# A two-layer gated-branch block with routed experts on one core: inputs laid out beforehand, router weights loaded at the layer's start, two more buffers for expert weights

## The chip, the core and the metric

The kernel runs on one core of one Trainium2 chip. The core has a matrix engine (PE, with its weight loads shown as PEld), three engines for element-wise work (DVE, ACT and POOL), a queue engine (SP) that issues most DMAs, and 16 DMA engines that move data between the chip's memory (DRAM) and the on-chip memory of 128 partitions. ACT and POOL can issue DMAs too; each issuing engine has its own queue. The metric is the device time of one execution in microseconds.

## The reference, cut to what matters

There are 256 latent tokens and 256 context tokens of width 1024, all in float32, and two layers. The second layer drops the context stream after its attention keys and values.

```python
for l in range(DEPTH):                                   # 2
    sh1, sc1, g1, sh2, sc2, g2 = split(silu(c) @ w_mod[l] + b_mod[l], 6)      # w_mod 1024 x 6144
    csh1, ..., cg2             = split(silu(c_ctx) @ w_mod[l] + b_mod[l], 6)
    p_x = modulate(rmsnorm(x, norm1_g[l]), sh1, sc1) @ w_in[l]                # w_in 1024 x 5376
    p_c = modulate(rmsnorm(ctx, norm1_g[l]), csh1, csc1) @ w_in[l]
    # three mixers on slices of p: windowed attention with a sink, depthwise conv of width 31, pooling
    x = x + g1 * merge_branches(...)                     # w_attn_o, w_conv_o, w_pool_o, gates, w_out
    # (context likewise in layer 0)
    h = modulate(rmsnorm(x, norm2_g[l]), sh2, sc2)
    aff = softmax(h @ w_router[l])                       # 16 experts
    g, idx = top_k(aff.T, 32)                            # each expert takes its 32 best tokens
    ye = (silu(xe @ w_e_gate) * (xe @ w_e_up)) @ w_e_down * g     # each matrix 1024 x 1024
    x = x + g2 * scatter_add(ye, idx)
return rmsnorm(x, final_norm_g)
```

The experts' weights are 16 x 3 x 4 MB per layer, 403 MB of the 530 MB that the kernel reads in all.

## The kernel before, in words

A tile framework keeps an order of priorities (mostly that of the program text), plans every engine's queue when the program is built, and places the waits. An instruction can therefore stand earlier in its queue than in the text, if its buffer was free in the planner's own clock. Each queue then runs strictly in order on the chip.

**Start.** L124 to L150 load the constants, c and c_ctx, the tokens and the small vectors, as rows which PE then turns into columns (L153, and `small_operands`, L168). `mod_first` (L371) computes shift and scale of layer 0's first norm in two halves of 512 columns each. A half reads four 1 MB tiles from the ring, each filled by two DMAs (L378) whose pieces are 2 KB long. Half 0 is needed for channels 0 to 3 of the normalized tokens, half 1 for channels 4 to 7 (`modulated`, L412).

**Mixers.** Weights come through a ring of five 1 MB buffers, tag `w` (`ring`, L103). `win` (L509) and `load` (L207) fetch 256 columns of w_in, in pieces of 1 KB; `qload` (L402) fetches q's columns in two DMAs with pieces of 512 bytes. ACT and DVE (or POOL) split each tile into a high and a low part (`split`, L214; buffers `ws`), and PE multiplies in three products (`mm3`, L490: its lines 494, 495 and 497). The later modulation matrices (`mod_group`, L227) are pumped in between these units. `layer_vectors` (L287) brings the conv taps and the sink. `merge` (L737) reads the three output projections, `project` (L863) reads w_out and adds the result to the stream.

**Routing.** `route` (L902) turns the tokens, multiplies them with the router weights `wr` and, for the part of the shift, with constant vectors (L905); softmax, top 32 by four rounds of max and replace, and one-hot matrices follow. `wr` stands in the tile `rt_` of the expert stage's memory (L852), is cleared by POOL (L854) and filled by two DMAs from ACT's queue (L855), in pieces of 64 bytes.

**Experts.** Each expert takes twelve loads of 1 MB: four of gate, four of up, four of down, in that order (`seq`, L331), with 8 KB per partition in one piece. `slot` (L310) hands out buffers in a fixed cycle: in layer 0 x0 to x3, once `y`, the five of the ring, two each of B, `A0`, `A1` and two of `ws`, 16 at first; in layer 1 also `xc`, `x4` and D, 19 in all. `prefetch` (L335) is called for two loads behind the attention of layer 1 and for two ahead of routing in both layers; `eload` (L352) asks for the others. PE computes gate and up (L1095), turns the hidden values (L1110), multiplies with down (L1118 in layer 0, L1123 in layer 1), and adds to the stream every four (layer 0) or two (layer 1) experts (L1140).

```python
order = ["x0", "x1", "x2", "x3"]
if last:
    order = ["xc", "A1"] + order + ["x4"] + ["w"] * RB + ["B", "B", "A0", "D", "D", "ws", "ws"]
else:
    order += ["w"] * RB + ["B", "B", "A0", "A1", "ws", "ws"]
```

## Time and profile before

| | us |
|---|---|
| median of 3 runs | 1751.48 (1750.38 to 1753.07) |
| the profiled execution | 1752.59 |
| its span in the trace | 1750.7 |
| PE busy | 1533.1 (88%) |
| DVE, ACT, POOL busy | 668.5, 408.1, 235.3 |
| DMA of the SP queue, share of 16 engines | 77.3% |
| mean granted PE clock | 0.955 |

Busy times are the union of an engine's instructions; a matmul's end is modelled, so a full PE is not PE at its peak. A float32 matmul has two records in the trace. The page cuts the span into 40 slices of 43.8 us; a digit is a busy share in tenths. A DMA share can exceed 1 a little, since packets overlap at their edges. In the chain of waits each piece is what released the next.

### The profile page before, as it was taken

Reading aid. Unit: us, or ns where it says so; the run is one execution under the profiler, and the core shown is the slowest. Engines: PE = TensorE matmul, PEld = TensorE weight load, DVE = VectorE, ACT = ScalarE, POOL = GpSimd, SP = SyncE. Lnnn points to the kernel's source line nnn. Section 1 sums busy time; section 2 is a strip of 40 time slices with the busy share of each in tenths; the row PEclk is TensorE's granted clock in tenths of the full one; section 3 lists DMA queues with packets and bytes.
Section 4 is the critical chain, followed back from the end, with each engine's and each line's share of the span. In section 5 each row is a group of like instructions: output and inputs, shape, how many; then the busy total and the mean of one; then the engine's idle time right before and its main releaser. Section 6 shows DMA issues by size and latency. Waiting matters only on the chain.

```text
span 1750.7 us, 19617 instructions
## 1 busy us (share of the span) xinstructions
PE 1533.1 (88%) x7794; PEld 825.5 (47%) x7794; DVE 668.5 (38%) x1145; ACT 408.1 (23%) x760; POOL 235.3 (13%) x242
## 2 busy tenths in 40 slices
PE   4999989999999999999999899999879676777675
PEld 2665567888654433433333376789743111111111
DVE  2568993352552221121211368966432110111011
ACT  2455312232432100000000267434321000000001
POOL 1300430154640000000000020235100000000000
PEclk9999999999999999999999999999989989888898
DMA  9833537244637999999999845776689999999996
GB/s 307 274 127 126 163 107 238 78 166 149 223 138 282 422 421 421 420 421 421 421 420 421 302 177 174 230 239 206 248 334 420 421 421 421 421 421 421 421 421 245
DMA packets 136347, 529.94 MB, mean 303 GB/s; under 512 B 11920, under 2 KB 60496, under 8 KB 83008
## 3 DMA queue, kind: packets, MB, share of 16 engines
q1 hardware_dynamic: 131456, 526.25, 77.3%
q10 hardware_dynamic: 4128, 1.97, 0.4%
q8 instruction: 61, 1.00, 0.2%
q0 software_dynamic: 672, 0.47, 0.1%
q14 instruction: 30, 0.25, 0.0%
HBM read 527.60 MB, written 1.05 MB: 302 GB/s over the span
## 4 chain that ended last, share of the span: by engine, by line
DMA 39%; PE 27%; DVE 3%; POOL 2%; ACT 1%; issue 1%; POOLq 0%; ACTq 0%; SPq 0%; DVEq 0%
DMA we<-in_w_e_up_dram 25%; DMA we<-in_w_e_down_dram 13%; PE mm L1095 7%; PE mm L1118 4%; PE mm L495 2%; PE mm L494 2%; PE mm L497 2%; PE mm L1005 2%; PE mm L890 2%; DMA rt<-in_w_router_dram 1%; DMA w<-in_w_in_dram 1%; POOL ws L224 1%; PE ax L1140 1%; PE md L244 1%; PE ax L643 1%
## 5 line engine op out<-in xcount | busy, mean ns | idle before, releaser
L1095 PE MATMUL mm<-we,xeT 128*64 128x512 f32 (+1 forms) x2048 | 424.3, 628 | 86.7 <-DMA we<-in_w_e_up_dram 65.8
L1095 PEld LDWEIGHTS mm<-we,xeT 128*64 128x64 f32 (+1 forms) x2048 | 126.9, 125 | 375.7 <-issue 186.9
L494 PE MATMUL mm<-hh,ws 128*128 128x512 f32 (+1 forms) x672 | 221.2, 348 | 1.9 <-ACT hh L428 1.9
L495 PE MATMUL mm<-hl,ws 128*128 128x512 f32 (+1 forms) x672 | 218.8, 345 | 0.2 <-DVE hl L429 0.2
L223 ACT ACTIVATE ws<-w 128x1024 fp32r<-128x1024 f32 x132 | 139.1, 1058 | 275.5 <-PE mm L497 164.3
L1102 DVE TENSOR_TENSOR hm<-si,mm 64x512 f32<-64x512 f32 x48 | 33.1, 690 | 437.4 <-ACT si L1100 436.6
L1100 ACT ACTIVATE si<-mm 64x512 f32<-64x512 f32 x48 | 28.4, 591 | 718.6 <-PE mm L1095 718.6
L476 DVE SCALAR_TENSOR_TENSOR acc<-up,dw,acc 128x512 f32<-128x512 f32 (+1 forms) x240 | 154.5, 689 | 0.9
L224 DVE TENSOR_TENSOR ws<-w,ws 128x1024 fp32r<-128x1024 f32 x94 | 123.6, 1320 | 72.9 <-ACT ws L223 72.7
L494 PEld LDWEIGHTS mm<-hh,ws 128*128 128x128 f32 x672 | 127.9, 191 | 31.5 <-issue 10.7
L1118 PE MATMUL mm<-we,hT 128*64 128x512 f32 x512 | 132.9, 652 | 8.4 <-ACT hT L1113 8.4
L495 PEld LDWEIGHTS mm<-hl,ws 128*128 128x128 f32 x672 | 128.0, 191 | 18.1 <-issue 2.3
L497 PE MATMUL mm<-hh,ws 128*128 128x512 f32 (+1 forms) x672 | 134.3, 340 | 0.5 <-DVE ws L224 0.4
L224 POOL TENSOR_TENSOR ws<-w,ws 128x1024 fp32r<-128x1024 f32 x38 | 96.1, 2534 | 213.6 <-ACT ws L223 213.6
L497 PEld LDWEIGHTS mm<-hh,ws 128*128 128x128 f32 x672 | 107.0, 189 | 17.4 <-issue 2.4
L1060 POOL COPY sg<-kc 48x128 f32<-48x128 f32 (+1 forms) x16 | 4.4, 287 | 757.1 <-PE ax L1140 754.7
L1130 DVE TENSOR_TENSOR Y<-mm,G 32x512 f32<-32x512 f32 x64 | 43.9, 687 | 144.1 <-PE mm L1118 143.3
L1123 PE MATMUL mm<-we,hT 128*32 128x512 f32 x512 | 85.0, 782 | 8.5 <-DMA we<-in_w_e_down_dram 4.6
L1118 PEld LDWEIGHTS mm<-we,hT 128*64 128x64 f32 x512 | 40.2, 149 | 92.4 <-issue 76.7
L1140 PE MATMUL ax<-Y,sg 128*128 128x512 f32 x128 | 58.7, 604 | 8.8 <-DVE Y L1133 6.4
L1110 PE MATMUL ax<-kc,hm 64*128 64x64 f32 x192 | 32.1, 290 | 29.2 <-DVE hm L1102 28.9
L1133 DVE TENSOR_TENSOR Y<-mm,G 64x512 f32<-64x512 f32 x32 | 22.0, 689 | 89.6 <-PE mm L1123 89.2
(274 smaller groups left out, 1639.0 us busy)
## 6 DMA issues: line engine op xcount, KB each, us to landing
we<-in_w_e_gate_dram SPq DMA_DIRECT2D x128, 1024.0 KB, 19.8
we<-in_w_e_up_dram SPq DMA_DIRECT2D x128, 1024.0 KB, 19.8
we<-in_w_e_down_dram SPq DMA_DIRECT2D x120, 1024.0 KB, 19.8
w<-in_w_mod_dram SPq DMA_DIRECT2D x40, 1024.0 KB, 5.0
w<-in_w_in_dram SPq DMA_DIRECT2D x38, 1024.0 KB, 5.3
w<-in_w_out_dram SPq DMA_DIRECT2D x12, 1024.0 KB, 6.2
w<-in_w_mod_dram SPq DMA_DIRECT2D x16, 512.0 KB, 9.5
we<-in_w_e_down_dram SPq DMA_DIRECT2D x16, 512.0 KB, 12.4
```

Of the source, the lines that this page charges most:

```text
L223: nc.scalar.activation(h, src, AF.Copy)
L224: (nc.gpsimd if eng == "p" else nc.vector).tensor_sub(lw, src, h.bitcast(F32))
L476: nc.vector.scalar_tensor_tensor(acc[:, ch], up[:, ch, :, k:k + 256], dw[:, 4 * k + ch:4 * k + ch + 1], acc[:, ch], op0=ALU.mult, op1=ALU.add)
L494: nc.tensor.matmul(ps, wh[:, k, :], ah[:, k, :n], start=k == 0, stop=False)
L495: nc.tensor.matmul(ps, wh[:, k, :], al[:, k, :n], start=False, stop=False)
L497: nc.tensor.matmul(ps, wl[:, k, :], ah[:, k, :n], start=False, stop=k == nk - 1)
L890: nc.tensor.matmul(pss[t], a, b, start=k == 0 and st == 0, stop=k == 7 and st == 2)
L1095: nc.tensor.matmul(o, xeT[k // 4][:, k % 4, e, :], w[:, kk, 512 * f:512 * f + 512], start=k == 0, stop=k == 7)
L1118: nc.tensor.matmul(pd[64 * h:64 * h + 64, :], hT[:, 64 * k:64 * k + 64], rhs, start=k == 0, stop=k == 7)
L1123: nc.tensor.matmul(pd[o:o + 32, :], hT[:, c0:c0 + 32], rhs, start=k < 2, stop=k >= 6)
L1130: nc.vector.tensor_mul(Y[b0:b0 + 32, s, cols], pd[rw, :], G2[l][rw, :])
L1140: nc.tensor.matmul(po, sgs[s][:, t * 128:(t + 1) * 128], Y[:, s, cols], start=True, stop=True)
```

## The change

All inputs are rearranged on the host into the form in which the chip's memory holds them. The tables, c, c_ctx and all small vectors are one table `kcv`; identity, masks and counting matrices come in bfloat16 as `kb16`; the tokens are two loads with 8 KB per partition; the taps and the sink are one load; w_in, w_attn_o, w_conv_o, w_pool_o, w_out and the first 2048 columns of layer 0's w_mod lie in blocks of 1 MB with 8 KB rows; biases are repeated over the partitions. The transposes and casts on the chip which made columns of rows are gone. The second half of `mod_first` no longer uses the ring but the B buffer and two new buffers of 1 MB, e0 and e1. These two enter the cycle of expert buffers: 18 in layer 0, 21 in layer 1. Two expert loads are called for behind the attention in layer 0 (ahead of routing before) and four in layer 1 (two before). The router weights have a tile of their own, `wr`, one per layer in turn, and are called for at the layer's start in one load of 1 KB rows. POOL issues no DMA any more, and the memory set aside for its descriptors is cut (`dynamic_dma_scratch_size`).

```diff
+    kcv = np.concatenate(
+        [kc, columns(a["c"], 8), columns(a["c_ctx"], 8), columns(a["norm1_g"], 8), pair]
+        + [columns(a[n], 4) for n in ("conv_dw_b", "conv_ln_g", "conv_ln_b", "pool_scale")], axis=1)
...
+    w_mod0 = a["w_mod"][0, :, :2048].reshape(4, 2, 128, 2, 2, 512).transpose(4, 0, 2, 1, 3, 5)
+    bm = np.repeat(a["b_mod"].reshape(L, 3, 4, 512), 32, axis=2)
...
+    w_in = a["w_in"].reshape(L, 8, 128, 21, 256).transpose(0, 3, 2, 1, 4).copy()
+    q = a["w_in"][:, :, :512].reshape(L, 8, 128, 2, 2, 128).transpose(0, 4, 2, 1, 3, 5)
+    w_in[:, 0:2] = q.reshape(L, 2, 128, 8, 256)
...
+    w_router = np.zeros((L, 128, 4, 2, 32), np.float32)
+    w_router[..., :NE] = a["w_router"].reshape(L, 4, 128, 2, NE).transpose(0, 2, 1, 3, 4)
...
-    nc.sync.dma_start(crow[0:8], c.rearrange("o (k p) -> (o k) p", p=128))
-    nc.sync.dma_start(crow[8:16], c_ctx.rearrange("(k p) -> k p", p=128))
...
+    for s in range(2):
+        nc.sync.dma_start(XS[s].rearrange("p t d -> p (t d)"), tok[s])
...
         def layer_vectors():
-            drow = t2("drow", 128)[0:4 * CK, :]
-            nc.sync.dma_start(drow, conv_dw[l].rearrange("k (a p) -> (k a) p", p=128))
-            pw = bank("ax")
-            nc.tensor.transpose(pw[:, 0:4 * CK], drow, ident[:4 * CK, :4 * CK])
-            nc.vector.tensor_scalar(dw, pw[:, 0:4 * CK], 0.5, None, op0=ALU.mult)
-            nc.sync.dma_start(sink, attn_sink[l].unsqueeze(0).to_broadcast([128, NH]))
+            nc.scalar.dma_start(dws, cols[l])
+            nc.vector.tensor_scalar(dw, dw, 0.5, None, op0=ALU.mult)
             nc.vector.tensor_scalar(nsink, sink, -1.0, None, op0=ALU.mult)
...
-        order = ["x0", "x1", "x2", "x3"]
+        order = ["x0", "x1", "x2", "x3"] if last else ["e0", "e1", "x0", "x1", "x2", "x3"]
         if last:
-            order = ["xc", "A1"] + order + ["x4"] + ["w"] * RB + ["B", "B", "A0", "D", "D", "ws", "ws"]
+            order = ["xc", "A1", "e0", "e1"] + order + ["x4"] + ["w"] * RB + ["B", "B", "A0", "D", "D", "ws", "ws"]
...
             for k2 in range(4):
-                w = ring().rearrange("p (k a n) -> p k a n", k=2, a=2)
-                for kk in range(2):
-                    k = 2 * k2 + kk
-                    nc.sync.dma_start(w[:, kk], w_mod[0, k * 128:(k + 1) * 128, 0:2048].rearrange(
-                        "p (a n) -> p a n", a=2)[:, :, hf * 512:(hf + 1) * 512])
+                w = (mw.pop(0) if mw else ring()).rearrange("p (k a n) -> p k a n", k=2, a=2)
+                nc.sync.dma_start(w.rearrange("p k a n -> p (k a n)"), w_mod0[hf, k2])
...
         def qload(u):
-            tv = ring().rearrange("p (k h n) -> p k h n", k=8, h=2)
-            for h in range(2):
-                nc.sync.dma_start(tv[:, :, h, :], w_in[l].rearrange("(k p) n -> p k n", p=128)[
-                    :, :, OQ + 256 * h + 128 * u:OQ + 256 * h + 128 * u + 128])
-            return tv
+            return load(w_in[l, u], "p (k h n) -> p k h n", k=8, h=2)
...
             next(first)
-            small_operands()
+            mbias = t2("mbias")
+            nc.scalar.dma_start(mbias, b_mod[0, 0])
+            nc.scalar.dma_start(bt, kb16)
             next(first, None)
             qw = [qload(0)]
             for d in range(4):
                 modulated(d, (0, 1))
+            b8 = big("B", "wm")
+            mw += [b8[:, :2048], b8[:, 2048:], half("e0", "wm"), half("e1", "wm")]
             for _ in mod_first(1, "ax"):
                 pass
         else:
             qw = [qload(0)]
-        nc.sync.dma_start(rope, rope_in.rearrange("p (a t) -> p a t", a=2))
+        wr = P0.tile([128, 8, 32], F32, tag="wr", name="wr")
+        nc.scalar.dma_start(wr.rearrange("p k e -> p (k e)"), w_router[l])
+        nc.sync.dma_start(rope.rearrange("p a t -> p (a t)"), rope_in)
...
-        if last:
-            prefetch(2)
+        prefetch(4 if last else 2)
...
-        wr = rt_[:, 0:256].rearrange("p (k e) -> p k e", k=8)
-        nc.gpsimd.memset(wr, 0.0)
-        for kk in range(2):
-            nc.scalar.dma_start(wr[:, kk::2, 0:NE], w_router[l].rearrange(
-                "(i p k) e -> p k i e", p=128, k=2)[:, kk])
...
-        prefetch(2)
+        if last:
+            prefetch(2)
...
-                nc.gpsimd.dma_start(frow, final_norm_g.unsqueeze(0))
+                nc.scalar.dma_start(frow, final_norm_g.unsqueeze(0))
...
-    nc = _bacc.Bacc("TRN2", target_bir_lowering=False, num_devices=1)
+    nc = _bacc.Bacc("TRN2", target_bir_lowering=False, num_devices=1,
+                    dynamic_dma_scratch_size=64)
```

## Rows read from the trace of the kernel before

**Rows 1.** The page: the span in 40 slices, busy tenths, then GB/s

```profile
PE   4999989999999999999999899999879676777675
DMA  9833537244637999999999845776689999999996
GB/s 307 274 127 126 163 107 238 78 166 149 223 138 282 422 421 421 420 421 421 421 420 421 302 177 174 230 239 206 248 334 420 421 421 421 421 421 421 421 421 245
```

**Rows 2.** The chain of waits in order of time: start us, us, what

```profile
559.67 13.73 PE mm L1095 x64
...
586.24 13.73 PE mm L1095 x64
...
672.77 13.80 PE mm L1095 x64
...
696.42 12.94 PE mm L1095 x60
...
731.04 19.81 DMA we<-in_w_e_up_dram
...
1239.97 20.01 DMA rt<-in_w_router_dram
...
1308.88 14.03 DMA we<-in_w_e_up_dram
...
1702.47 19.86 DMA we<-in_w_e_up_dram
```

**Rows 3.** Timeline of the start: start us, us, engine, line, what [idle before <-releaser]

```profile
8.03 7.15 SPq L378 DMA_DIRECT2D w<-in_w_mod_dram  x8
...
15.23 8.79 SPq L405 DMA_DIRECT2D w<-in_w_in_dram  x2
...
27.97 1.08 PE L382 MATMUL md<-w,cst 128*32 128x256 f32 x8 [0.33 <-DMA w<-in_w_mod_dram]
...
42.91 1.50 PE L382 MATMUL ax<-w,cst 128*32 128x256 f32 x24
```

**Rows 4.** Stretches of the start: us, busy by engine, granted clock, DMA share, GB/s

```profile
8.00:16.00 8.00, 1.63 (x11) 0.72 (x11) 1.70 (x4) 3.10 (x6) 4.46 (x8) 1.00 0.95 304
16.00:24.00 8.00, 3.50 (x32) 0.76 (x32) 1.42 (x2) 0.00 (x0) 0.52 (x1) 1.00 1.07 289
...
30.00:36.00 6.00, 4.44 (x28) 3.62 (x26) 4.36 (x12) 3.43 (x6) 0.00 (x0) 1.00 1.05 387
```

**Rows 5.** Timeline of SP's queue: expert loads of layers 0 and 1

```profile
370.25 0.57 SPq L348 DMA_DIRECT2D we<-in_w_e_gate_dram  x1
...
509.49 0.33 SPq L348 DMA_DIRECT2D we<-in_w_e_up_dram  x1
536.15 0.33 SPq L348 DMA_DIRECT2D we<-in_w_e_gate_dram  x1
...
1240.62 29.73 SPq L348 DMA_DIRECT2D we<-in_w_e_down_dram  x4
...
1273.69 0.43 SPq L348 DMA_DIRECT2D we<-in_w_e_gate_dram  x1
1296.77 0.33 SPq L348 DMA_DIRECT2D we<-in_w_e_up_dram  x1
```

**Rows 6.** Timeline of layer 1's routing: PE's longest stop

```profile
1260.03 1.07 PE L905 MATMUL ax<-modT,rt 128*32 128x128 f32 x14 [6.25 <-DMA rt<-in_w_router_dram]
```

**Rows 7.** Stretches of layer 1's routing, with the columns of Rows 4

```profile
1250.00:1260.00 10.00, 3.46 (x16) 2.37 (x14) 5.04 (x6) 3.46 (x6) 0.00 (x0) 0.92 0.78 307
1260.00:1270.00 10.00, 9.97 (x54) 7.53 (x55) 1.92 (x2) 1.66 (x2) 0.62 (x1) 0.74 0.01 2
1270.00:1280.00 10.00, 7.19 (x33) 4.39 (x31) 3.79 (x5) 1.93 (x5) 2.64 (x5) 0.83 0.89 356
...
1290.00:1300.00 10.00, 10.00 (x83) 6.29 (x85) 2.29 (x7) 3.30 (x10) 0.00 (x0) 0.87 0.36 129
```

**Rows 8.** Waits of ACT from 1000 to 1240 us: total, times, longest

```profile
ACT ws L223 <- DMA w<-in_w_in_dram: 7.8, 3, 3.8
```

174 lines of the change are left out of this document (70 added, 104 removed).

## The prediction

> **What bounds the kernel now.** I read the page's slices first. DMA runs at 9 tenths or more, about 421 GB/s, in two long blocks, the expert stages of layer 0 (slices 14 to 22) and layer 1 (slices 31 to 39); elsewhere it moves 78 to 334 GB/s while PE is nearly full [rows 1]. So no one engine bounds the whole span, and each stage must be read by itself. The chain of waits, in order of time, says which: PE in layer 0 until about 731 us, expert loads from there to the end of that stage, a mix of PE, ACT and DVE in layer 1's mixers, one 20.01 us piece of router weights at 1239.97, then expert loads from 1308.88 to 1722 [rows 2]. A load in the blocks lands 19.8 us after its issue with eight in flight, one per 2.49 us, which is 1 MiB at 421 GB/s [rows 1, 2].
>
> This gives the rule for the whole sum. In an expert stage the last byte arrives at (start of the unbroken stream) + 2.49 us x (loads not yet made by then). An edit pays if it moves that start earlier or takes a load out of the stream. In layer 0 an edit ahead of the stage pays only as far as PE moves, since PE is nearly full from 48 us on [rows 1].
>
> **The change, part by part.**
>
> *Start.* Layer 0's first modulation needs x, the constants and four tiles of w_mod. Its last group of matmuls waits for its load and ends at 27.97 + 1.08 = 29.05 us [rows 3]. The eight half-tile loads are issued only from 8.03 us, behind thirteen others, and two w_in loads in 512-byte pieces join them at 15.23 [rows 3]. The engines are full, yet move 304 GB/s from 8 to 16 us and 289 from 16 to 24; from 30 to 36 us, when 2 KB pieces are left nearly alone, it is 387; the 8 KB pieces of the expert blocks make 421 [rows 1, 4]. After the change, what lies ahead of the last tile in issue order is 0.22 MB table, 2.1 MB tokens, 4.2 MB weights, and 0.46 MB of bias and mask on ACT's queue: 6.97 MB. At 421 GB/s that is 16.6 us, from about 2 us on, plus 0.5 us to land: 19.1. The last 1 MB tile holds two groups of 1.08 us, so the first modulation ends at 21.3 and gains 7.8 us. At 387 GB/s it gains 6.4, at 304 only 1.5. I take 7.5, near the 421 end, since all large pieces are 8 KB. The second half now has its own four buffers; its last tile is 4.2 + 1.05 MB further (w_in's first), 12.5 us later, at 31.6. PE today takes the last 24 matmul records of that half at 42.91 [rows 3], 13.9 us behind the first half's end; so the data does not bind it (35.2 would be its turn) and the 7.5 us carry through. If PE's order were free to follow the data the gain could reach 10. PE then stays nearly full up to the experts [rows 1], so the shift arrives there. The dozen transposes, casts and copies that fall away lie beside the wait for the first tile and count nothing; uncovered, at the 0.27 us of one matmul in the 1.08 us group (an estimate), they would be 3 us. POOL's DMA issues that go to ACT's queue were beside the same wait.
>
> *Two more buffers, layer 0.* Sixteen expert loads are issued between 370.25 and 509.49; then every buffer is full, and SP waits until expert 0 frees one at 536.15 [rows 5]. The stream is unbroken only from there. With e0 and e1 loaded early, two of 192 loads leave it: 2 x 2.49 = 5.0 us. PE does not take over: with the gather of the second token half between, it does an expert in 586.24 - 559.67 = 26.6 us, and 696.42 - 672.77 = 23.7 without, against 12 x 2.49 = 29.9 us of loads [rows 2]. The two loads go out earlier, into a stretch where PE waits for no load. I take 5.0; 3 if new holes open at the stream's head.
>
> *Router weights early.* In layer 1 the weights are issued after their cleared tile, at 1239.5 us, behind expert loads; the 20.01 us follow [rows 2]. They come in 64-byte pieces, 1024 of them, 64 for each of 16 DMA engines. If each piece waits for one 8 KB piece of the other queue (8192 B at 421/16 GB/s = 0.311 us), that is 19.9 us: the row is explained. But not 20 us are won. PE works on output projection meanwhile and stands still only for 6.25 us, until 1260.03 [rows 6]. [...] The stop also holds back the last weight split of that projection, and SP with four loads, x4 over 29.73 us from 1240.62 [rows 5]: the DMA engines stand at 0.01 in 1260 to 1270 [rows 7]. Without the stop the last split, the remaining seven loads and expert 0 all move by 6.2 + 2.0 = 8.2 us. Bounds: 3, if the next release is late, and 12, if DMA's hole there closes nearly altogether. In layer 0 the same load lands in time; nothing there.
>
> *Two more buffers, layer 1.* Nineteen loads are out by 1273.69; then SP waits for expert 0 until 1296.77, and DMA is at 0.36 in 1290 to 1300 [rows 5, 7]. The stage is bound by its loads from the first expert on. Two loads fewer in the stream: 5.0 us. Zero at the other end, if e0 and e1 are filled so late that they only replace loads.
>
> *The rest.* In layer 1's mixers ACT waited 7.8 us in three pieces for w_in [rows 8]. Its 1 KB pieces lie between the 512 B and 2 KB of the start, so a 1 MB load takes between 3.6 us (289 GB/s) and 2.7 (387) and would take 2.5: 0.2 to 1.1 us less [rows 4]. But two extra expert loads, 2.5 us each, now share this stretch. Bounds -5 (a loss) to +4; I take +1, near the upper price of one shortened load. layer_vectors now waits on one ACT-queue load: ACT's activations stand behind its issue, DVE's splits behind its landing, and PE behind both. An issue takes 0.33 to 0.57 us [rows 5], covered by PE's full stretch; uncovered it is that and one load's turn, 2.5 us a layer, within those bounds. The merged bias loads take three issues away from ACT five times; ACT isn't the bound. final_norm_g goes from POOL's queue to ACT's at the end, 4 KB beside the last expert's loads; late, it would cost one turn, 2.5 us. The order on all queues is planned anew: -4 to +4, taken as 0.
>
> Sum: 7.5 + 5.0 + 8.2 + 5.0 + 1.0 = 26.7 us. The profiled execution took 1752.59 us (span 1750.7 and 1.9 around); less 26.7 it is 1725.9. It lay 1.1 above the median of the runs, 1751.48, so I predict 1725.
>
> [...] The rows say that pieces of 512 B and 2 KB keep the engines full and still move less than 8 KB pieces: 289 and 387 against 421 GB/s [rows 1, 4]. If piece size did nothing, the start would gain by issue order alone, 1.5 to 6.4 us for 7.5, and the sum would be 1731 to 1726 for 1725; its low end is rival 1. [...]
>
> **The rivals.**
> 1. The start stays slow. It is led by many loads at once on cold queues, not by piece size, and keeps the 304 GB/s of 8 to 16 us. For it: x and ctx come in 4 KB pieces, and the first 16 us never hold 421. Against: 386 or more as soon as small pieces are gone. The first term is 1.5: 1731.
> 2. The router wait is replaced. Another wait of the same stage comes last: the ring buffers that SP's four loads wait for, or the route's chain of small DVE steps. Then the 8.2 is near 0: 1733. For it: SP's own wait is longer than PE's. Against: the splits it waits for stood behind PE's stop.
> 3. More is won. The DMA engines' idle time of layer 1's routing closes altogether: by their shares 2.2 + 9.9 + 1.1 us in 1250 to 1280 and 6.4 in 1290 to 1300 [rows 7], 19.6 us in place of 8.2, so 1714. For it: the engines have work to fetch. Against: the second hole is SP's wait for expert 0, which moves with PE.
> 4. Slower. The two streams make up 174 + 171 loads. Where their addresses in memory and on the chip are new, a load could take longer than 2.49 us; from 26.7 / 345 = 0.077 us more (3%) the gain is gone, and at 5% it is 43 - 27 = 16 us slower: 1767. Against: all slices of both layers show 420 to 422 GB/s, with different buffers and weights [rows 1].
> 5. It does nothing: the planner places the early loads where the late ones stood, and PE's order at the start doesn't follow. 1750.
>
> **How the numbers follow.** Forecast 0.60, rival 1 0.12, rival 2 0.12, rival 3 0.07, rival 4 0.05, rival 5 0.04. Faster or slower by 0.2% (3.5 us) is about what a measurement can tell from no change. Forecast and rivals 1 to 3 lie over 0.2% faster: 0.91. Rival 5: 0.04 the same. Rival 4: 0.05 slower. The range holds the forecast with its bounds and rivals 1 to 3, 1711 to 1738; outside are rivals 4 and 5 and the tails of bounds that fail together.
>
> **What would show it.** First modulation done at 20 to 23 us, PE full from about 41. Layer 0: SP's pause before expert 0 still there, 18 loads ahead, the stage's last load some 12 us earlier. Layer 1: no wait of the route's first matmuls on router weights, the granted clock above 0.9 in those 10 us, the DMA hole there half as long, 21 loads ahead, stream at 421 GB/s. Wrong if the stream is below 415, if PE meets waits for w_in in layer 1, or if either stage starts with fewer loads ahead.

## The result, and the profile after

The changed kernel takes 1721.95 us (median; 1721.91 to 1722.63), the kernel before beside it 1751.39 (1750.38 to 1753.07): 0.9832 of its time, 95% interval 0.9815 to 0.9849, or 29.4 us less. Forecast were 1725 us and a range of 1711 to 1738. The profiled execution spans 1720.2 us, 30.5 less than the 1750.7 of before; the sum had 26.7. Timed again later on another occasion, the same kernel took 1724.57 us (1721.20 to 1728.61) beside 1751.08, 0.9845 of the time (0.9830 to 0.9860): 26.5 us less. Which of the two differences belongs to the change is the last question below.

The page of the changed kernel, its span in 40 slices, against [rows 1]:

```profile
PE   6999989999999999999999899999979766666675
DMA  9733445244536999999999864566789999999996
GB/s 398 276 122 129 147 147 202 78 152 165 220 147 267 421 421 421 421 420 421 421 422 420 334 240 178 201 232 226 278 334 420 421 421 421 421 421 421 422 421 272
```

The first slice moves 398 GB/s instead of 307. The two long blocks are the same blocks at the same 421 GB/s, entered earlier.

The chain of waits, in order of time (start us, us, what), against [rows 2]:

```profile
1225.94 13.63 PE mm L859 x60
...
1243.49 6.59 PE mm L859 x28
...
1266.47 6.24 PE mm L974 x32
1272.70 7.00 PE mm L1065 x64
...
1288.42 17.10 DMA we<-in_w_e_up_dram
1305.54 19.86 DMA we<-in_w_e_up_dram
```

Where the router weights stood with 20.01 us, PE's output projection stands now, then the gather (L974) and expert 0 (L1065). From 1288 us on it is expert loads, one per 2.49 us (eight in 19.86).

The timeline of the start (us, us, engine, line, what, idle before), against [rows 3]:

```profile
2.11 5.06 SPq L372 DMA_DIRECT2D w<-in_w_mod_dram  x4
...
20.47 1.87 PE L375 MATMUL md<-w,cst 128*32 128x256 f32 x16 [0.56 <-DMA w<-in_w_mod_dram]
...
33.61 1.93 PE L375 MATMUL ax<-wm,cst 128*32 128x256 f32 x32
```

The first half of the first modulation ends at 22.34 us (20.47 + 1.87), 6.7 earlier, and the second at 35.54 (33.61 + 1.93), 8.9 earlier than 44.41 (42.91 + 1.50).

SP's queue in the two expert stages, against [rows 5]:

```profile
501.84 0.33 SPq L344 DMA_DIRECT2D we<-in_w_e_up_dram  x1
528.50 0.33 SPq L344 DMA_DIRECT2D we<-in_w_e_gate_dram  x1
...
1013.12 1.21 SPq L344 DMA_DIRECT2D we<-in_w_e_gate_dram  x2
...
1250.92 25.73 SPq L344 DMA_DIRECT2D we<-in_w_e_down_dram  x4
```

Before expert 0 of layer 0, SP's pause is still there, 26.7 us, now with 18 loads out instead of 16. In layer 1 the extra loads go out at 1013, early in the mixers, and 21 are out when expert 0 gives the next buffer free.

Stretches of layer 1's routing, with the columns of [rows 4], against [rows 7]:

```profile
1240.00:1250.00 10.00, 10.00 (x60) 7.73 (x52) 3.60 (x4) 3.00 (x5) 0.00 (x0) 1.00 0.61 223
1250.00:1260.00 10.00, 4.51 (x23) 2.07 (x21) 5.46 (x13) 2.16 (x6) 2.64 (x5) 0.72 1.01 425
1260.00:1270.00 10.00, 4.74 (x24) 4.15 (x24) 6.80 (x25) 3.28 (x10) 0.00 (x0) 0.50 0.87 363
1270.00:1280.00 10.00, 10.00 (x85) 4.85 (x84) 0.82 (x2) 1.53 (x4) 0.00 (x0) 0.93 0.44 164
```

The stretch in which DMA stood at 0.01 is gone; what is left of the hole is spread over two. PE's clock is no better: 0.50, which is the lower of the two levels in the trace's clock records (1 and 0.5), in a stretch in which PE is busy for 4.74 us of 10 and the route's chain on DVE for 6.80.

The same events in both traces give the sum in parts. Each entry is the time won between one event and the next, from starts of instructions (the last gate and up matmul counts by its end); the last column is the second trace of the changed kernel (e11 below).

| part, from event to event | forecast | changed | again |
|---|---|---|---|
| to SP's first release at expert 0 of layer 0 (536.15 to 528.50) | 7.5 | 7.65 | 7.60 |
| to the last gate and up matmul of layer 0 (two buffers) | 5.0 | 5.07 | 5.70 |
| to layer 1's first transposes | 0 | 1.63 | 0.00 |
| to the output projection of layer 1 (its mixers) | 1.0 | -0.85 | -3.12 |
| to SP's first release at expert 0 of layer 1 (router weights) | 8.2 | 8.67 | 8.63 |
| to the last gate and up matmul of layer 1 (two buffers) | 5.0 | 6.76 | 5.21 |
| to the end | 0 | 1.54 | -0.17 |
| sum | 26.7 | 30.47 | 23.85 |

### The profile page after: what moved, and what is told of

Read it like the earlier page. It is cut to its first block, busy times and chain, and to the rows that moved or that the text cites. A ratio compares the mean times of both kernels' runs of the same rounds, so it can differ in the third digit from the quotient of the medians.

```text
span 1720.2 us, 19498 instructions
## 1 busy us (share of the span) xinstructions
PE 1515.4 (88%) x7788; PEld 822.1 (48%) x7788; DVE 672.5 (39%) x1137; ACT 407.7 (24%) x760; POOL 229.7 (13%) x234
## 5 line engine op out<-in xcount | busy, mean ns | idle before, releaser
L1065 PE MATMUL mm<-we,xeT 128*64 128x512 f32 (+1 forms) x2048 | 414.4, 620 | 78.6 <-DMA we<-in_w_e_up_dram 59.7
L1065 PEld LDWEIGHTS mm<-we,xeT 128*64 128x64 f32 (+1 forms) x2048 | 125.0, 125 | 361.7 <-issue 191.5
L1070 ACT ACTIVATE si<-mm 64x512 f32<-64x512 f32 x48 | 28.4, 591 | 693.8 <-PE mm L1065 693.8
L1088 PE MATMUL mm<-we,hT 128*64 128x512 f32 x512 | 126.1, 625 | 8.4 <-ACT hT L1083 8.4
L1030 POOL COPY sel<-kc 48x128 f32<-48x128 f32 (+1 forms) x16 | 4.6, 287 | 806.4 <-DVE hm L1072 434.6
L1110 PE MATMUL ax<-Y,sg 128*128 128x512 f32 x128 | 62.5, 636 | 8.0 <-DVE Y L1103 6.4
```

Of the source, the lines that this page charges most:

```text
L1065: nc.tensor.matmul(o, xeT[k // 4][:, k % 4, e, :], w[:, kk, 512 * f:512 * f + 512], start=k == 0, stop=k == 7)
L1088: nc.tensor.matmul(pd[64 * h:64 * h + 64, :], hT[:, 64 * k:64 * k + 64], rhs, start=k == 0, stop=k == 7)
L1110: nc.tensor.matmul(po, sgs[s][:, t * 128:(t + 1) * 128], Y[:, s, cols], start=True, stop=True)
```

## The experiments

The theory was the prediction's: each expert stage ends at the start of its unbroken stream plus 2.49 us a load; the router weights cost a stop of 6 us and some clock; the start is a matter of bytes and piece size. The rivals: the buffers only replace loads; the stop has other causes; the start was won by issue order; and parts of the 30.5 us are no part of the change. "Changed" is the changed kernel, "before" the kernel before.

### e1: without the two buffers

```diff
-        order = ["x0", "x1", "x2", "x3"] if last else ["e0", "e1", "x0", "x1", "x2", "x3"]
+        order = ["x0", "x1", "x2", "x3"]
...
-            order = ["xc", "A1", "e0", "e1"] + order + ["x4"] + ["w"] * RB + ["B", "B", "A0", "D", "D", "ws", "ws"]
+            order = ["xc", "A1"] + order + ["x4"] + ["w"] * RB + ["B", "B", "A0", "D", "D", "ws", "ws"]
...
-            if once and nload[0] == 6:
+            if once and nload[0] == 4:
...
-        prefetch(4 if last else 2)
+        if last:
+            prefetch(2)
...
-        if last:
-            prefetch(2)
+        prefetch(2)
         rt = route(0)
```

> The changed kernel, with the two buffers e0 and e1 taken out of the cycle of expert loads (they still serve the second half of the first modulation). Theory (an expert stage ends at the start of its unbroken stream plus 2.49 us for every load not yet made): 16 loads ahead in layer 0 and 19 in layer 1, each stage 2 x 2.49 = 5.0 us longer, so 10 us slower in all, 1732; expert 0 of either layer starts when it did. Rival A (the loads ahead only replace others, or the holes ahead of the stage close by themselves): 0 to 5 us slower. Rival B (the early loads cost the mixers more than they seem to: the 1.0 us that layer 1's mixers lost in the changed kernel comes back without them): 9 us slower, and layer 1's mixers end 1 us earlier from their start.

Measured: 1733.99 us (1730.21 to 1735.00), 0.9906 of before (0.9890 to 0.9923), 12.0 us over the changed kernel's first median and 9.4 over its second (e11), 7.9 over the first profiled span (1728.1 and 1720.2). SP's queue in its trace, which ends the loads ahead at 499.70 and 1252.32 and goes on at expert 0:

```profile
499.70 0.33 SPq L344 DMA_DIRECT2D we<-in_w_e_up_dram  x1
526.35 0.33 SPq L344 DMA_DIRECT2D we<-in_w_e_gate_dram  x1
...
1275.71 0.33 SPq L344 DMA_DIRECT2D we<-in_w_e_up_dram  x1
```

From these releases to the last gate and up matmul it takes 437.9 and 427.4 us, and 433.6 and 422.3 in the changed kernel: 4.3 and 5.1 longer. That is 2.1 and 2.6 us a load, and rival A falls. The other traces say the same for layer 1: from SP's first release to the first of the last 14 gate and up matmuls it takes 425.5 to 425.7 us in the five traces without the two buffers (before, e1, e4, e10, e12) and 420.2 to 420.8 in the nine with them. Expert 0 of layer 0 comes 2.15 us earlier, of layer 1 1.1 later; the clock is at its lower level for 3.4 us between the first modulation and expert 0 of layer 0 here, and for 10.2 in the changed kernel, and half of that difference, 3.4 us (an estimate, at the half microsecond of e4 for each), is more than what came back. Rival B's return of 1.0 us in the mixers can't be read: from layer 1's first transposes to the output projection they take 235.8 us here and 236.5 in the changed kernel, but 238.8 when it was run again.

### e2: router weights late, in 64-byte pieces

```diff
-        wr = P0.tile([128, 8, 32], F32, tag="wr", name="wr")
-        nc.scalar.dma_start(wr.rearrange("p k e -> p (k e)"), w_router[l])
         nc.sync.dma_start(rope.rearrange("p a t -> p (a t)"), rope_in)
...
         rt_ = MO.tile([128, RT], F32, tag="rt", name="rt")
+        wr = rt_[:, 0:256].rearrange("p (k e) -> p k e", k=8)
+        nc.gpsimd.memset(wr, 0.0)
+        for kk in range(2):
+            nc.scalar.dma_start(wr[:, kk::2, 0:NE], w_router[l].rearrange(
+                "(i p k) e -> p k i e", p=128, k=2)[:, kk])
```

> The changed kernel, with the router weights loaded late again, as in the kernel before: at the output projection of each layer, on ACT's queue behind a clearing, in 64-byte pieces. Theory (the stop of the route in layer 1 is this load, and it costs 6.2 us of waiting and about 2 us at the lower clock): expert 0 of layer 1 starts 8 to 9 us later, layer 0 does not change, the whole is 8.5 us slower, 1730. Rival A (the stop in layer 1 has other causes, the start and the two buffers moved it): 0 us. Rival B (all 20 us of the landing are paid): 20 us slower, 1742.

Measured: 1729.45 us (1726.09 to 1730.78), 0.9875 (0.9858 to 0.9892). Its timeline and one stretch:

```profile
1236.97 0.38 PE L877 MATMUL ax<-modT,rt 128*32 128x128 f32 x2 [1.04 <-DMA rt<-in_w_router_dram]
1242.78 1.07 PE L877 MATMUL ax<-modT,rt 128*32 128x128 f32 x14 [5.42 <-DMA rt<-in_w_router_dram]
```

```profile
1240.00:1250.00 10.00, 7.22 (x42) 5.25 (x43) 0.69 (x1) 0.60 (x1) 0.61 (x1) 0.66 0.07 27
```

PE's stop on the router weights is back (5.42 us, and 1.04 before two earlier matmuls), and so is the hole in DMA, 0.07 of its share. From the first matmul of the output projection to SP's first release at expert 0 it takes 57.7 us; 57.9 before, 49.2 and 49.3 in the two traces of the changed kernel. So the one load is worth 8.4 us, forecast 8.2, and both rivals fall.

### e3: router weights late, in 1 KB pieces

```diff
-        nc.scalar.dma_start(wr.rearrange("p k e -> p (k e)"), w_router[l])
...
         rt_ = MO.tile([128, RT], F32, tag="rt", name="rt")
+        wr = rt_[:, 0:256].rearrange("p (k e) -> p k e", k=8)
+        nc.scalar.dma_start(rt_[:, 0:256], w_router[l])
```

> The changed kernel, with the router weights loaded late, at the same place and on the same queue as in the kernel before, but as one load of 1 KB pieces (128 pieces, 8 for each DMA engine) and without the clearing. Theory (each piece waits for one 8 KB piece of SP's queue, 0.311 us): it lands 8 x 0.31 = 2.5 us and a start of some 2 us after its issue, 4 to 5 us in all, instead of 13.7 to 20 us; the route hardly waits, and the whole is 0 to 2 us slower than the changed kernel, 1722 to 1724. Rival (a late load stands behind the 8 MB that SP's queue has in flight, whatever its pieces): it lands after about 20 us, and the whole is 8.5 us slower, 1730.

Measured: 1721.87 us (1719.18 to 1728.93), 0.9841 (0.9814 to 0.9868), no difference to the changed kernel; 48.9 us from the projection to expert 0. The load, and who waits for it:

```profile
L826 ACTq DMA_DIRECT2D rt<-in_w_router_dram x1: 334/334/334, 1229.6 to 1229.6; - x1
...
  POOL rt L829: 7.5, 1
```

It lands 7.4 us after its issue, not 4.5 and not 20; only POOL waits, and PE doesn't. The trace's DMA records, counted, show what the time is made of (number of pieces whose transfer began in that microsecond; SP's queue and ACT's):

```
e2, 64-byte pieces              e3, 1 KB pieces
us     SP 8192 B   ACT 64 B     us     SP 8192 B   ACT 1024 B
1226      52          36        1233      45          33
1227      48          61        1234      46          57
1228      47          51        1235      47          36
1229      51          53        1236      51           2
1230      50          62        1237      52           0
...
1236      52          51
1237      45         239
```

In e2 some 50 pieces of 8 KB and 48 to 63 of 64 B begin in each microsecond from 1227 to 1236: in number one for one, although the large ones hold 128 times the bytes. Only the last 430 small ones go faster, most of them in 2 us from 1237. The 1024 small ones so take some 13 us, but for a few that lag behind; 128 of 1 KB take 3. Before the first piece there are 3.5 us in either kernel (1222.4 to 1225.97, 1229.6 to 1233.08), which the expectation had at 2. What made the load dear was the number of its pieces, not its lateness. Nor was it the clearing, which e3 leaves out as well: in e2, e3 and before alike the load is issued 0.6 to 0.7 us behind the projection's first matmul.

### e4: router weights early, nothing else

The kernel before, with a tile of its own for the weights and the one early load.

```diff
+        wr = P0.tile([128, 8, 32], F32, tag="wr", name="wr")
+        nc.scalar.dma_start(wr.rearrange("p k e -> p (k e)"), w_router[l])
         nc.sync.dma_start(rope, rope_in.rearrange("p (a t) -> p a t", a=2))
...
-        wr = rt_[:, 0:256].rearrange("p (k e) -> p k e", k=8)
-        nc.gpsimd.memset(wr, 0.0)
-        for kk in range(2):
-            nc.scalar.dma_start(wr[:, kk::2, 0:NE], w_router[l].rearrange(
-                "(i p k) e -> p k i e", p=128, k=2)[:, kk])
```

> The kernel before, with one part of the change alone: the router weights are loaded at the start of each layer, in 1 KB pieces, into a tile of their own. Theory (the part is worth what it was in the whole, 8 to 9 us, and independent of the two buffers): 1742.5 to 1743.5, expert 0 of layer 1 starts 8 to 9 us earlier from the end of the mixers. Rival A (without more buffers ahead, SP's pause and not the route sets expert 0): 0 to 3 us. Rival B (one more load at the start, where DMA is the limit, takes back what the route gains, 0.3 us at most): no difference to the theory that could be seen.

Measured: 1739.86 us (1737.23 to 1743.65), 0.9939 (0.9919 to 0.9960), 11.6 us less than before. From the projection to expert 0 it takes 47.7 us, 10.2 less. That the expectation's 8 to 9 is passed can be the clock's doing: the trace's clock records show the lower level for 20.5 us of that stretch before, 17.1 in the changed kernel and 10.2 here, and each microsecond of it that PE works through costs about half (3.42 us against 1.92 for the same matmuls, under e11). How much of it PE worked through was not measured. So the part stands alone; it needs no buffers ahead (rival A).

### e5: the first modulation in 2 KB pieces

```diff
-                nc.sync.dma_start(w.rearrange("p k a n -> p (k a n)"), w_mod0[hf, k2])
+                for kk in range(2):
+                    k = 2 * k2 + kk
+                    nc.sync.dma_start(w[:, kk], w_mod[0, k * 128:(k + 1) * 128, 0:2048].rearrange(
+                        "p (a n) -> p a n", a=2)[:, :, hf * 512:(hf + 1) * 512])
```

> The changed kernel, with the eight tiles of the first modulation loaded in 2 KB pieces, two loads for each tile, as in the kernel before; buffers and order stay. Theory (2 KB pieces move 387 GB/s where 8 KB pieces move 421): 4.2 MB take 10.8 us instead of 10.0 in each half, so the first half ends about 1 us later and the second about 2 us later, and DMA shows 385 to 400 GB/s between 8 and 24 us; the whole 1 to 2 us slower. Rival A (pieces of 512 B and more run at full rate, the issue order alone made the start faster): 421 GB/s stays, 0 us. Rival B (twice the loads at eight in flight leave too little under way): below 340 GB/s, the halves 3 and 6 us later.

Measured: 1723.96 us (1720.56 to 1728.23), 0.9845 (0.9823 to 0.9866). Stretches of its start:

```profile
8.00:16.00 8.00, 3.61 (x28) 0.83 (x32) 3.13 (x6) 3.19 (x6) 1.83 (x4) 1.00 1.04 387
16.00:24.00 8.00, 6.38 (x47) 2.15 (x40) 0.98 (x7) 0.00 (x0) 0.00 (x0) 1.00 1.04 398
```

and its last matmuls of the second half:

```profile
36.97 1.50 PE L378 MATMUL ax<-wm,cst 128*32 128x256 f32 x24
```

387 and 398 GB/s against 422 and 422 in the changed kernel: the rate is as forecast. The first half still ends at 22.10, 0.2 us before the changed kernel's. Its last load is half a tile, so that 1.08 us of matmuls stand behind it instead of 1.87, which gives back what the rate takes. The second half ends 2.9 us later (38.47), 1 more than expected, with PE's clock at 0.84 to 0.88 from 24 to 36 us: one stretch of 3.4 us at the lower level, which can cost up to 1.7 (an estimate, half of it as under e4).

### e6: q in 512-byte pieces

```diff
-            return load(w_in[l, u], "p (k h n) -> p k h n", k=8, h=2)
+            for h in range(2):
+                nc.sync.dma_start(tv[:, :, h, :], w_q[l].rearrange("(k p) n -> p k n", p=128)[
+                    :, :, 256 * h + 128 * u:256 * h + 128 * u + 128])
```

> The changed kernel, with the two q tiles of each layer loaded in 512-byte pieces, two loads each, as in the kernel before. Theory (the 512-byte pieces are what held the start at 289 to 304 GB/s, and what cost the end of layer 0 its 1.6 us): the first half of the first modulation ends where it did; the second, behind the first q tile, ends 1 to 2 us later; from the last gate and up tile of layer 0 to the first transposes of layer 1 it takes 28.4 us instead of 26.7; 2 to 4 us slower in all. Rival A (they hide): 0 us. Rival B (the 1.6 us at the end of layer 0 is the clock's, not the load's): the second half 1 to 2 us later, the end of layer 0 as now.

Measured: 1724.23 us (1721.56 to 1727.72), 0.9846 (0.9827 to 0.9865).

```profile
8.00:16.00 8.00, 2.77 (x24) 1.08 (x28) 3.04 (x6) 3.49 (x8) 2.21 (x4) 1.00 1.02 422
16.00:24.00 8.00, 5.96 (x49) 2.38 (x42) 0.69 (x4) 0.00 (x0) 0.00 (x0) 1.00 1.09 363
```

The 512-byte pieces do cost rate, in the few microseconds that they take: 363 GB/s over 16 to 24 us, 295 in the two in which they are alone. The second half ends 0.7 us later. Expert 0 of layer 0 comes 1.2 earlier, with 3.4 us at the lower clock ahead of it instead of 10.2, so this says nothing of the load. The end of layer 0 takes 28.2 us here; but it takes 28.4 in e7, whose q loads are those of the changed kernel. Rival B is right: that row is no matter of the q load.

### e7: the second half through the ring

```diff
-            b8 = big("B", "wm")
-            mw += [b8[:, :2048], b8[:, 2048:], half("e0", "wm"), half("e1", "wm")]
```

> The changed kernel, with the second half of the first modulation loaded through the ring of five buffers, as in the kernel before, in place of four buffers of its own. Theory (DMA is the limit from 2 us on, and the ring's tiles come free one by one as the first half is multiplied, before the stream runs out): the second half ends 0 to 1 us later, the whole unchanged. Rival (SP waits for the ring: the second half's loads are issued only when the first half's matmuls are done, and DMA has a hole): the second half ends 4 to 8 us later, a hole in DMA between 20 and 30 us, the whole as much slower.

Measured: 1725.43 us (1723.49 to 1727.68), 0.9852 (0.9836 to 0.9869). The second half ends at 35.70 us instead of 35.54, and DMA moves 425 GB/s from 16 to 24 us and 421 from 24 to 30. There is no hole: the four buffers of its own bring the first modulation nothing that can be seen (0.2 us).

### e8: the rest of w_in in 1 KB pieces

```diff
-            return load(w_in[l, c0 // 256], "p (k n) -> p k n", k=8)
+            nc.sync.dma_start(tv, w_raw[l].rearrange("(k p) n -> p k n", p=128)[:, :, c0:c0 + 256])
```

> The changed kernel, with all other tiles of w_in (k, v, conv, pooling and gates: 19 loads of 1 MB a layer) loaded in 1 KB pieces, as in the kernel before. Theory (a load gets 0.2 to 1.1 us longer, and most lie beside a full PE): the mixers of each layer are 0 to 2 us longer, 1 to 3 us in all. Rival A (no difference, since DMA is half idle there): 0 us. Rival B (the weight splits wait for every second tile, and each 1 MB load is paid in full in layer 1, where ACT waits for them): 5 to 10 us.

Measured: 1721.84 us (1720.25 to 1724.75), 0.9834 (0.9814 to 0.9854). Waits of ACT in layer 1's mixers (total, times, longest), in the changed kernel:

```profile
ACT ws L227 <- DMA w<-in_w_in_dram: 8.5, 3, 4.0
```

and in e8:

```profile
ACT ws L227 <- DMA w<-in_w_raw_dram: 17.2, 5, 6.0
```

The waits double, from 8.5 to 17.2 us, and the mixers take 235.7 us, against 236.5. ACT isn't what they wait for. Rival A holds, and the forecast's +1 for these loads was nothing.

### e9: the start in a better order

```diff
-            nc.scalar.dma_start(dws, cols[l])
+            nc.sync.dma_start(dws, cols[l])
...
-                nc.sync.dma_start(w.rearrange("p k a n -> p (k a n)"), w_mod0[hf, k2])
+                if k2 < 3:
+                    nc.sync.dma_start(w.rearrange("p k a n -> p (k a n)"), w_mod0[hf, k2])
+                else:
+                    for kk in range(2):
+                        nc.sync.dma_start(w[:, kk].rearrange("p a n -> p (a n)"),
+                                          w_mod0[hf, k2][:, 1024 * kk:1024 * kk + 1024])
...
-            nc.scalar.dma_start(bt, kb16)
             for _ in mod_first(1, "ax"):
                 pass
+            nc.sync.dma_start(bt, kb16)
...
-        nc.scalar.dma_start(wr.rearrange("p k e -> p (k e)"), w_router[l])
         nc.sync.dma_start(rope.rearrange("p a t -> p (a t)"), rope_in)
+        nc.sync.dma_start(wr.rearrange("p k e -> p (k e)"), w_router[l])
```

> The changed kernel, with three small loads of the start (masks, router weights, convolution taps: 0.40 MB) taken from ACT's queue, where they go out first, and put on SP's behind the sixteen tiles that the first modulation needs, and with the last tile of each half loaded in two loads of 4 KB pieces. Theory (DMA is the limit from 2 us on, so what is ahead of the last tile in bytes is paid; the group of matmuls behind the last tile is 1.93 us, 1.08 us for half a tile): the last load of the first half lands 0.9 us earlier, its matmuls end 0.8 us sooner behind it, the first half ends at 20.6 us instead of 22.3, the second as much earlier, and the whole is 1.7 us faster than the changed kernel. Rival A (the small loads only fill gaps between large pieces): the landing does not move, 0.8 us. Rival B (the order of all queues is planned anew and takes it back): the first half is earlier, expert 0 of layer 0 is not.

Measured: 1723.33 us (1720.21 to 1723.60), 0.9830 (0.9817 to 0.9844), beside e11's 0.9845 (0.9830 to 0.9860). The end of the first half:

```profile
20.02 0.81 PE L380 MATMUL md<-w,cst 128*32 128x256 f32 x8 [0.17 <-DMA w<-in_w_mod_dram]
```

It ends at 20.83, 1.5 us before the changed kernel, of which 0.45 is the landing and the rest the half tile. The second half ends 0.9 us later, and expert 0 of layer 0 comes 0.8 earlier. Rival B holds in part: about half is taken back before it counts, and the interval doesn't tell this kernel from the changed one.

### e10: before, with the bias on ACT's queue

```diff
-                for a in range(2):
-                    o = 1024 * a + 512 * f
-                    nc.gpsimd.dma_start(
-                        mbias[f][64 * a:64 * a + 64], b_mod[0, o:o + 512].rearrange(
-                            "(g n) -> g n", g=2).unsqueeze(1).to_broadcast([2, 32, 256]))
+                nc.scalar.dma_start(mbias[f], b_first[f])
```

> The kernel before, with one thing of its start changed: the bias of the first modulation comes laid out, in two loads of 1 KB pieces on ACT's queue, not as four broadcasts on POOL's. Theory (between 14 and 24 us, while POOL's queue moves the broadcasts, a 2 KB piece takes 107 to 131 ns, and 84 to 88 ns before and after; it is this that held the start to 289 GB/s, and not the 512-byte q pieces, which come from 24 us on): 16 to 24 us shows about 380 GB/s, the first half ends 2 to 2.5 us earlier, near 26.7, and the whole is 2 to 2.5 us faster than the kernel before. Rival A (the mix of 512-byte and 2 KB pieces sets the rate, as the prediction said): 290 GB/s stays, 0 us. Rival B (the loads ahead of the w_mod tiles set it, since SP issues the first only at 8.03 us): the rate rises, the last tile lands as before, 0 us.

Measured: 1747.51 us (1744.88 to 1749.60), 0.9978 (0.9968 to 0.9988). Its start, with its last matmuls of either half:

```profile
2.00:8.00 6.00, 0.26 (x1) 0.18 (x1) 1.38 (x7) 1.38 (x5) 0.40 (x3) 1.00 0.77 240
8.00:16.00 8.00, 1.26 (x11) 0.72 (x11) 2.29 (x6) 3.60 (x8) 1.81 (x4) 1.00 0.93 295
16.00:24.00 8.00, 5.87 (x47) 1.00 (x40) 0.73 (x2) 0.00 (x0) 0.00 (x0) 1.00 1.05 388
```

```profile
25.52 1.08 PE L382 MATMUL md<-w,cst 128*32 128x256 f32 x8 [0.30 <-DMA w<-in_w_mod_dram]
...
40.44 1.50 PE L382 MATMUL ax<-w,cst 128*32 128x256 f32 x24
```

16 to 24 us moves 388 GB/s where it moved 289 [rows 4], and the first half ends at 26.60, 2.5 us earlier. The theory holds. While a quarter of a megabyte of bias went by POOL's broadcasts, the other pieces were slower: the DMA records of before show a 2 KB piece at 127 ns (median, 16 to 20 us), and at 84 ns from 8 to 14 us. The interval, 0.12 to 0.32%, holds the 2.5 us.

### e12: the same, with the small vectors behind

```diff
     tokens(0)
-    nc.sync.dma_start(n2row, norm2_g.rearrange("l (i c) -> (l i) c", c=256))
-    for o, ap in ((VN1, norm1_g), (VCB, conv_dw_b), (VLG, conv_ln_g),
-                  (VLB, conv_ln_b), (VPS, pool_scale)):
-        r = rows(ap)
-        nc.sync.dma_start(vrow[o:o + r.shape[0]], r)
     tokens(1)
...
     def small_operands():
+        nc.sync.dma_start(n2row, norm2_g.rearrange("l (i c) -> (l i) c", c=256))
+        for o, ap in ((VN1, norm1_g), (VCB, conv_dw_b), (VLG, conv_ln_g),
+                      (VLB, conv_ln_b), (VPS, pool_scale)):
+            r = rows(ap)
+            nc.sync.dma_start(vrow[o:o + r.shape[0]], r)
```

This comes on top of e10's edit.

> The kernel before, with the bias of the first modulation laid out and on ACT's queue, and beside that the six loads of small vectors moved on SP's queue behind the eight loads of the first modulation's first half. Theory (the rest of what the start gained is a hole: with eight loads in flight, the six small ones keep SP from issuing the second half of the tokens and the tiles of w_mod until they land, and DMA moves 240 GB/s from 2 to 8 us and 295 from 8 to 16, where it could move about 400): SP issues the first tile of w_mod near 4 us, 2 to 8 us shows over 350 GB/s, and the matmuls of the first half end 4 to 4.5 us earlier than with the bias alone, near 22.5 instead of 26.6, within 0.5 us of the changed kernel though all pieces are 2 and 4 KB. Rival A (the pieces of 2 and 4 KB at the start hold the rate down): under 350 GB/s stays, and the first half ends 1 us earlier at most. Rival B (the vectors, now behind, hold up the step after the first half): the matmuls end earlier, the second half and expert 0 of layer 0 do not.

Measured: 1747.21 us (1741.82 to 1748.82), 0.9972 (0.9956 to 0.9987).

Stretches of its start, SP's queue in it, and its last matmuls of either half:

```profile
2.00:8.00 6.00, 0.25 (x1) 0.18 (x1) 1.38 (x7) 1.52 (x6) 0.39 (x3) 1.00 0.93 311
8.00:16.00 8.00, 3.24 (x24) 0.63 (x24) 2.83 (x4) 3.44 (x6) 1.82 (x4) 1.00 1.04 393
```

```profile
3.96 9.67 SPq L378 DMA_DIRECT2D w<-in_w_mod_dram  x8
```

```profile
22.11 1.08 PE L382 MATMUL md<-w,cst 128*32 128x256 f32 x8 [0.22 <-DMA w<-in_w_mod_dram]
...
38.52 0.64 PE L382 MATMUL ax<-w,cst 128*32 128x256 f32 x8 [0.57 <-DMA w<-in_w_mod_dram]
```

SP issues the first tile of w_mod at 3.96 us instead of 8.66 in e10, the rate rises from 240 to 311 and from 295 to 393 GB/s, and the first half ends at 23.20, another 3.4 us earlier; 4 to 4.5 were expected, as 2 to 8 us did not reach 350. So of the 6.7 us that the changed kernel won at this event, 5.9 are had with no input laid out but the bias: 2.5 from POOL's broadcasts, 3.4 from six small loads that held SP's eight places: in e10 SP issues the last of them at 4.75 us and its next load only at 7.00. Eight is what the changed kernel's trace shows in the expert stages, where SP issues a load 0.06 us (median of 286) after the eighth before it has landed. The second half is 2.8 us earlier than in e10, so rival B fails there; but expert 0 of layer 0 comes 0.6 us later, with the clock at its lower level for 10.2 us ahead of it instead of 3.4, and by time e12 and e10 are the same.

The first half is not the whole of the start. One group of eight matmuls in the mixers (L497 at 212.37 us before) has no low clock ahead of it in before, e10, e12 and the changed kernel. It starts at 209.72 in e10, 207.08 in e12 and 204.21 in the changed kernel. There the two edits bring 5.3 of 8.2 us. The other 2.9 come behind the first half, and no run takes them apart: e5 and e6, which give pieces of 2 KB and 512 B back to the changed kernel, start the group 2.7 (with the one low stretch) and 0.7 us later. So piece size can be most of this third, but e12 also moves its small loads into that part, where DMA falls to 206 GB/s from 20 to 22 us.

### e11: the changed kernel once more

No edit.

> The changed kernel itself once more, for the spread between executions. Theory (the unplanned 1.6 us at the end of layer 0 and 3.1 us behind the last expert load come from stretches of 3.4 us at the lower clock, which fall elsewhere in every execution): some stretches lie elsewhere; from the last gate and up tile of layer 0 to the first transposes of layer 1 it takes either 26.7 or 28.4 us, and the time is 1720 to 1726. Rival (these gains belong to the change): 26.7 us, and 23.4 us from the last gate and up tile of layer 1 to the end, 1722.

Measured: 1724.57 us (1721.20 to 1728.61), 0.9845 (0.9830 to 0.9860). The ends of the two expert stages, first in the changed kernel's first trace:

```profile
960.00:970.00 10.00, 8.53 (x27) 3.21 (x24) 1.38 (x2) 1.78 (x3) 0.00 (x0) 1.00 1.05 401
...
1700.00:1710.00 10.00, 8.42 (x38) 2.33 (x35) 2.76 (x4) 1.45 (x4) 1.28 (x1) 1.00 0.36 135
```

and in its second:

```profile
960.00:970.00 10.00, 8.53 (x22) 3.10 (x21) 1.38 (x2) 1.78 (x3) 0.00 (x0) 0.83 1.05 404
...
1700.00:1710.00 10.00, 7.78 (x34) 1.80 (x27) 0.84 (x2) 0.97 (x2) 0.00 (x0) 0.75 0.72 264
```

In the first window it is the same work, with PE busy for 8.53 us, once at the full clock and once at 0.83. In the second the work lies 4.9 us further on in the first trace, so that the events have to be compared. From the last gate and up matmul of layer 0 to layer 1's first transposes it takes 26.7 us in the first trace and 28.4 in the second, and 28.4 before; the clock records hold no low stretch there in the first, one of 3.4 us in the others, which costs 1.7. In all fourteen traces it is 26.7 to 26.8 (five, none with a low stretch there) or 28.1 to 28.4 (nine, each with one of 3.4 us), whatever the edit. Behind the last gate and up matmul of layer 1 it takes 23.3 and 25.1 us, with 5.1 and 8.2 us of low clock. The last 14 gate and up matmuls of layer 1, before and in the first trace:

```profile
1722.37 3.42 PE L1095 MATMUL mm<-we,xeT 128*32 128x512 f32 x14 [1.47 <-DMA we<-in_w_e_up_dram]
```

```profile
1694.94 1.92 PE L1065 MATMUL mm<-we,xeT 128*32 128x512 f32 x14 [1.47 <-DMA we<-in_w_e_up_dram]
```

Before, 3.2 us of the 3.42 are at the lower level, in the first trace nothing, in the second trace 3.4 of 3.58. So the 1.63 and 1.54 us of the table, and 1.5 of the 6.76, are where the low clock fell in one execution, not the change.

## Why the prediction was right, point by point

**The total** was right: 26.7 us in the sum, 29.4 and 26.5 measured. With these three places where the clock fell taken out, the parts of the first trace give 25.8 (30.47 less 1.63, 1.54 and 1.5).

**Start, 7.5; measured 7.65 and 7.60.** The size was right, and in part by luck; its reason, piece size, made about a third of it at most. The step "the engines are full, yet move 304 GB/s from 8 to 16 us and 289 from 16 to 24" read [rows 4] as a matter of piece size. The DMA records say that the 512-byte q pieces move only from 24 us on, and that from 14 to 24 us POOL's broadcasts run; without them the rate is 388 (e10). From 8 to 16 us it was not the pieces either, though the share of DMA stood at 0.95: with the six small loads behind, pieces of 2 and 4 KB move 393 GB/s there (e12). Rival 1, "many loads at once on cold queues, not by piece size", was right that the pieces were not the first cause, and wrong that the start would then stay slow; that queues were cold no run shows. Piece size is worth what e5 and e6 show, 387 to 398 GB/s for 2 KB and 422 for 8 KB, and next to nothing in the first half's end; behind it, it can be most of the last 2.9 of 8.2 us (e12).

The sum itself met its number by two errors that cancel. The first half ended at 22.34 and not at 21.3: by count the last piece of 8 KB that the half needs, the 768th, ends at 19.64 us and not at 18.6, and PE starts 0.83 us behind it; no row gave the 0.5 that the sum took for that. So 6.7 us were won there and not 7.5, and the shift did not simply carry through: the second half won 8.9, of which 8.2 were left in the mixers (e12) and 7.65 at expert 0; where the rest went is open.

Weighed against this term was that piece size might do nothing, and the start gain by issue order alone. The runs disagree on the rate: 295 GB/s with 512-byte pieces alone (e6), 387 to 398 with 2 KB (e5), 422 with 8 KB. They agree only at the first half's end, which pieces of 2 KB and 512 B move by less than 0.3 us (e5, e6).

**Two buffers, 5.0 each; measured 5.07 and 6.76, again 5.70 and 5.21, and 4.3 and 5.1 by e1.** Right in mechanism and size; 1.5 of the 6.76 is the clock's. PE did not take over in either layer.

**Router weights, 8.2; measured 8.67, again 8.63, and 8.4 by e2.** Right in size and in the first term: PE's stop of 6.25 us [rows 6] is the 5.42 + 1.04 of e2. The piece for piece turn, worked out from one row as 64 x 0.311 us, is seen in the numbers of e2. That 19.9 us met the row's 20.01 so closely is luck: before the first piece there are 3.6 us (1239.5 to 1243.13 in the trace of before), and some 430 of the 1024 go faster at the end. Nor do the small pieces go in bursts: between 1227 and 1236 us of e2 never more than 10 of them on all engines together begin within 0.1 us, at 5.5 on average, though one takes 11 ns. What failed is the form of the second term. "Granted clock above 0.9 in those 10 us", 1260 to 1270 us of before with its 0.74 [rows 7], did not come: the low clock is still there, 0.72 and 0.50, during the route's chain on DVE, which nothing in the change touches. The 2.0 us of that term no run shows by itself. What the clock records show is the lower level for 20.5 us of the whole stretch before and for 17.1 now; half of the difference, 1.7 us, can be its worth (an estimate, as under e4).

**The hole in DMA at [rows 7]** was forecast half as long. By the DMA records no piece was under way for 5.6 us from 1259.4, for 4.5 from 1266.5, and again for 4.5 from 1291.9, ahead of expert 0's release; now it is 2.2 us from 1246.0, and 6.4 from 1269.1. In sum it is 8.6 us instead of 14.6. The hole at the stop shrank from 10.1 to 2.2 us, the one ahead of the release grew: there 21 loads are out and SP waits for expert 0, and it is the next thing to take away.

**The rest, +1; measured -0.85 and -3.12.** Wrong, and the bound of -5 was of use. e8 shows that w_in's pieces are worth nothing: its waits on ACT are covered. The loss is not shown to be the change's: the mixers take 235.7 us before, 236.5 and 238.8 in two traces of the changed kernel, with 3.4, 3.4 and 6.8 us of low clock. Of all traces with 3.4, the five without the extra loads take 234.7 to 235.8 us and the five with them 235.7 to 236.5. What of it belongs to the two extra loads stays open, up to 1 us.

**Rival 4**, a stream slower than 2.49 us a load, has no sign: 19.86 us for eight loads, 421 GB/s.

## What to carry to other kernels

Here a transfer on ACT's queue took turns with SP's large pieces one for one (some 50 of 8 KB and 48 to 63 of 64 B in a microsecond of e2; 1024 small pieces took some 13 us, 128 of 1 KB in e3 took 3): where that is so, count pieces, not bytes, and either load it early or lay it out in a few long rows (e2, e3). At the start of a kernel ask first what the loads ahead of the first needed tile do to the issue order and to the eight places in flight (six small loads held the first tile back from 3.96 to 8.66 us, e12 and e10), and which queue still runs broadcasts, which here made two thirds of the gain (5.3 of 8.2 us), and then about piece size. In a stage bound by its loads a buffer filled ahead was worth about one load's turn (2.1 to 2.9 us for 2.49), and before a gain of 1 to 2 us is believed, the granted clock of the same rows should be compared (one low stretch of 3.4 us made 1.7 us at the end of layer 0, e11).

## What the runs showed of the hardware that was not expected

- While broadcast loads ran on POOL's queue, a 2 KB piece of SP's queue took 127 ns instead of 84, and all engines together moved 289 GB/s instead of 388 (before and e10).
- The granted clock is at its lower level, 0.5, for 3.4 to 17.1 us on end, also in a stretch with PE busy at 8.53 of 10 us (0.83, e11). The places differ between two executions of the same kernel; three of them (the two stage ends and layer 1's mixers) make some 5 us of the 6.6 by which the two traces of the changed kernel differ.
- Beside SP's stream of 8 KB pieces a small load on ACT's queue moves its first piece 3.5 us after its issue, with pieces of 64 B and of 1 KB alike (e2, e3); at the start of the changed kernel, with little else under way, the first such load took 1.3 us (0.72 to 2.02).
